# The recurrence's outputs ahead of the last 96 query products, with closer levels

## The chip, the cores and the metric

The kernel runs on one core of a Trainium2 chip. Its time is the device time of one execution in microseconds (us). Five engines run side by side, each with its own queue of instructions in a fixed order: TensorE (PE, matrix products; its weight loads are listed as PEld), VectorE (DVE), ScalarE (ACT), GpSimd (POOL) and SyncE (SP, which here only issues transfers). They meet through semaphores: an instruction that waits holds up everything behind it on its own engine.

## The reference, cut to what matters

The program is one layer of a residual block on 256 tokens of width 1024: a SwiGLU feed-forward, a mixing stage with two branches, a cross attention to a memory, and a second feed-forward. The change lies in the mixing stage, of which these are the two branches:

```python
q_a, f_a, i_a, g_a, q_b, k_b, v_b, f_b, gates = jnp.split(h @ w_in[l], IN_OFFSETS, axis=-1)
o_a = hgrn2_chunkwise(q_a, f_a, i_a, lb_all[l])           # gated linear recurrence, 8 heads of 128
o_a = rmsnorm(o_a, hg_norm_g[l]) * jax.nn.silu(g_a)
o_b = fox_attention(q_b, k_b, v_b, f_b + fox_f_bias[l])   # softmax attention with a forget gate
...
# fox_attention: per block of 128 queries
s = jnp.einsum('bhqd,bhkd->bhqk', qi, k32) * scale
s = s + ci[..., None] - c[:, :, None, :]                  # c: running sum of log forget
p = jax.nn.softmax(jnp.where(kpos <= qpos, s, -jnp.inf), axis=-1)
```

The recurrence's output at a token is a sum over earlier tokens of a decayed query-key product times the input. The attention needs its own queries, keys, values and the running sum `c`.

## The kernel before, in words

Weights come as tiles of 128 x 1024. Each is split by `load_split` into a rounded part `hi` (a copy on ACT, line 136) and a remainder `lo` (a subtraction on DVE, line 137); a projection makes three products per block (hi x hi, hi x lo, lo x hi). Four tiles make a chunk. There are eight buffers each of `hi` and `lo`, two chunks, so a chunk's split can begin when the chunk two before it has been used.

Every product issued through `MM` is noted in a list `log`; transposes are not. `r0` is the length of that list before the gate projection. From `r0` follow, in program order, 144 products of the recurrence's gate (`g_a` with the forget logits, moving width 344), then four chunks of 96 products each (moving width 256): k_b and q_b for heads 0 to 3, k_b and q_b for heads 4 to 7, 528 in all. The column projections `proj_col2` fill one of two `mm` banks of PSUM with 48 products, and DVE empties it (line 996).

The recurrence is computed in nine levels with block sizes 0, 1, 2, 4, 8, 16, 32, 64 and 128. A level of each of two groups of four heads makes some small products into an `acc` bank (`products`), multiplies the running decays into q and k on DVE (`grow`, lines 915 to 925), and keeps the wanted part of the products (`keep`, by DVE below 32, by ACT from 32 on). A level's products read the q and k that the level before has left, and `grow` overwrites what the products have read. So the levels form a chain between PE and DVE.

The framework's planner sets the order on each engine from program order, priorities and data dependences. `with after(n)` gives the instructions inside high priority and places each of those on PE behind product `n` of the list. In this way the levels, which stand behind all 528 products in program order, are woven between them: the nine numbers of `R_AT` say behind which product, counted from `r0`.

Behind the 528 products, in program order and with no such mark, come the recurrence's outputs: for each half `h` of the tokens 8 or 16 products of the kept matrices with the inputs `iv` into two of the four `acc` banks, the norm (`rstd_x`: four squares on ACT for both halves, a chain of eight tiny operations each on DVE), and a multiplication into the gate `Gt` (line 1026). Then POOL fetches the running sums by broadcast (`cbc`, `cbm`, lines 1030 and 1034) and masks them (line 1036). These take buffers of a pool of 20 that the recurrence's q and k gave up. Then two transposes (line 1042) and a copy on DVE (line 1043) lay the running sums in columns, `ct`. Then `fox_scores` makes the attention's scores into two `tr` and four `acc` banks and the softmax, and the v_b projection follows on PE.

Of the kernel before, what the change touches and what calls it, by code (L numbers as in the profile page):

```python
# [16 lines left out]
P = 128  # L17
# [24 lines left out]
L_Y = 16  # L42
M_O = (24, 36)

R_AT = (18, 66, 114, 166, 226, 286, 346, 390, 430)

WARM = 8

# [29 lines left out]
def block_kernel(ctx: ExitStack, tc: tile.TileContext, wts, head_in, gf_in, x_in, mem_in, memT_in, cols, rows, fbias, masks, out):  # L78
    nc = tc.nc
    V, S, G, PE = nc.vector, nc.scalar, nc.gpsimd, nc.tensor  # L80
# [10 lines left out]
    def MM(*args, **kw):  # L91
        log.append(PE.matmul(*args, **kw).ins)  # L92

    @contextmanager
    def after(i):

        with tc.high_priority(), tc.issue_after(log[min(i, len(log) - 1)]):
            yield
# [3 lines left out]
    def nm(s):  # L102
        count[0] += 1
        return f"{s}_{count[0]}"

    def m4(shape, dt=F32, n="m"):
        return mp.tile(shape, dt, tag="m4", name=nm(n))

    def s1(n=1, dt=F32, name="s"):
        return sp.tile([P, n], dt, tag=f"s{n}", name=nm(name), bufs=16)  # L110

    def acc():
        return pp.tile([P, 512], F32, tag="acc", name=nm("acc"), bufs=4)
# [4 lines left out]
    def trp():  # L118
        return pp.tile([P, 512], F32, tag="tr", name=nm("tr"), bufs=2)
# [86 lines left out]
    ident = cp.tile([P, P], F32, name="ident")  # L206
# [52 lines left out]
    def rstd_x(src):  # L259

        s = s1(2, name="ss2")
        for j in range(2):
            ssq(s[:, j : j + 1], src[j])
        return rstd_of(s)
# [688 lines left out]
    r0 = len(log)  # L953
# [15 lines left out]
    cc = sp.tile([8, T], F32, tag="fz", name="cc", bufs=1)  # L969
# [32 lines left out]
    for li, m in enumerate(LEVELS + (64, 128)):  # L1002
        with after(r0 + R_AT[li]):
            for r in recs:
# [7 lines left out]


    OA = Pair()
    for h in range(2):
        ps = [acc(), acc()]
        for hd in range(8):
            g, i = hd // 4, hd % 4
            isl = slice(i * P, (i + 1) * P)
            o = ps[g][:, isl]  # L1020
            MM(o, ATs[g][:, i, h, :], iv[g][:, h, isl], start=True, stop=(h == 0))
            if h == 1:
                MM(o, A128s[g][:, i, :], iv[g][:, 0, isl], start=False, stop=True)
        r = rstd_x(ps)
        for j in range(2):
            V.scalar_tensor_tensor(out=Gt[h][:, j * 512 : (j + 1) * 512], in0=ps[j], scalar=r, in1=Gt[h][:, j * 512 : (j + 1) * 512], op0=ALU.mult, op1=ALU.mult)


    cbc = m4([P, 8, P], n="cbc")
    G.dma_start(cbc, cd[:, 0:P].partition_broadcast(P))  # L1030
    cbm = []
    for g in range(2):
# [2 lines left out]
        tv = t.rearrange("p h (b s) -> p (h b) s", b=2)  # L1035
        G.affine_select(out=tv, in_=tv, pattern=[[0, 8], [-1, P]], compare_op=ALU.is_ge, fill=BIG, base=0, channel_multiplier=1)
        cbm.append(t)

    ct = s1(16, name="ct")
    pc = trp()  # L1040
    for h in range(2):
        PE.transpose(pc[:, h * 8 : h * 8 + 8], cc[:, h * P : (h + 1) * P], ident[0:8, 0:8])
    V.tensor_copy(ct, pc[:, :16])

    ps_, pT0s, pT1s = {}, [], []

# [365 lines left out]
```

## Time and profile before

| what | us |
|---|---|
| median of three runs | 782.95 (782.57 to 785.86) |
| the profiled execution | 783.57 |
| its span in the profile | 781.8 |
| PE busy | 771.5 |
| DVE busy | 648.9 |
| ACT busy | 472.9 |
| POOL busy | 47.3 |

Times in a timeline count from the span's start. A row of a timeline has the start, the length, the engine, the line, the operation, what is written and read, the shape and how many instructions it stands for; in brackets, how long the engine stood idle before it and what ended that. A product on plain f32 operands is listed as two instructions. The first level after the gate's chunk begins is at 285 us, the last level's products end at 326, and the recurrence's outputs are made from 338 to 343.

### The profile page before, as it was taken

The page shows a single profiled execution, that of the slowest core. Times are in us where ns is not written, and L with a number is a line of the kernel's source. Part 1 is how long each engine was busy: PE and PEld are TensorE (multiplying, and loading weights), DVE is VectorE, ACT ScalarE, POOL GpSimd, SP SyncE. Part 2 cuts the span into 40 slices and gives each one's busy share as a digit, 9 for nine tenths or more (in the row PEclk, how much of TensorE's full clock was granted, in tenths as well). Part 3 has the DMA queues.
Part 4 walks back from the last instruction along what each step waited for, and adds up shares of the span by engine and source line. Part 5 has one row for each costly group of instructions (what it writes and reads, how often), then busy time and mean ns, then how long its engine had stood idle before and what let it go on. Part 6 is the DMA issues. An engine that isn't in the chain of part 4 may idle for free.

```text
span 781.8 us, 13108 instructions
## 1 busy us (share of the span) xinstructions
PE 771.5 (99%) x4984; PEld 666.7 (85%) x4984; DVE 648.9 (83%) x999; ACT 472.9 (60%) x711; POOL 47.3 (6%) x80
## 2 busy tenths in 40 slices
PE   9999999999999999999999999999999999999996
PEld 7888878888899999988888888999888888888885
DVE  7799999999887787778778886997787987888874
ACT  7666676577753445447675434744655767777752
POOL 0000000000121100110001221012110000000000
PEclk9999999999999999999999999999999999999999
DMA  9874648377686563673489999679865199789921
GB/s 344 286 261 160 217 162 308 108 255 283 259 296 227 191 218 110 201 272 120 140 291 335 378 344 342 223 271 381 337 213 191 64 343 387 275 296 339 329 92 55
DMA packets 57390, 193.60 MB, mean 248 GB/s; under 512 B 6248, under 2 KB 9712, under 8 KB 57328
## 3 DMA queue, kind: packets, MB, share of 16 engines
q1 hardware_dynamic: 48080, 159.60, 56.7%
q0 software_dynamic: 9104, 33.04, 11.8%
q8 instruction: 39, 0.64, 0.3%
q14 instruction: 23, 0.19, 0.1%
q10 hardware_dynamic: 144, 0.13, 0.0%
HBM read 174.92 MB, written 17.83 MB: 247 GB/s over the span
## 4 chain that ended last, share of the span: by engine, by line
PE 87%; DVE 8%; issue 3%; ACT 1%; DMA 1%; DVEq 0%; ACTq 0%; SPq 0%
PE mm L92 58%; PE acc L92 24%; PE tr L92 3%; DVE lo L156 2%; DVE lo L137 2%; PE tr L324 1%; PE tr L399 1%; DMA raw<-in_wts_dram 1%; DVE sum L469 1%; DVE wide L500 1%; DVE sum L487 0%; DVE sum L465 0%; ACT hi L155 0%; ACT hi L136 0%; PE tr L1082 0%
## 5 line engine op out<-in xcount | busy, mean ns | idle before, releaser
L137 DVE TENSOR_TENSOR lo<-raw,hi 128x1024 fp32r<-128x1024 f32 (+1 forms) x220 | 261.3, 1208 | 48.0 <-ACT hi L136 44.6
L136 ACT CAST hi<-raw 128x1024 fp32r<-128x1024 f32 (+1 forms) x220 | 222.6, 1035 | 94.6 <-PE mm L92 51.1
L92 PE MATMUL mm<-lo,hT 128*128 128x512 f32 (+1 forms) x424 | 161.6, 385 | 0.0
L92 PE MATMUL mm<-hi,hT 128*128 128x512 f32 (+1 forms) x424 | 161.2, 384 | 0.0
L92 PE MATMUL mm<-hi,lT 128*128 128x512 f32 (+1 forms) x424 | 160.9, 384 | 0.0
L92 PE MATMUL acc<-hi,act 128*128 128x512 f32 x352 | 113.2, 390 | 0.0
L92 PE MATMUL mm<-hT,lo 128*128 128x256 f32 x384 | 109.4, 285 | 0.0
L92 PE MATMUL mm<-hT,hi 128*128 128x256 f32 x384 | 108.9, 284 | 0.3 <-issue 0.3
L92 PE MATMUL mm<-lT,hi 128*128 128x256 f32 x384 | 108.9, 284 | 0.0
L92 PEld LDWEIGHTS mm<-hi,hT 128*128 128x128 f32 x424 | 79.6, 188 | 15.1 <-ACT hT L285 0.5
L92 PEld LDWEIGHTS mm<-hi,lT 128*128 128x128 f32 x424 | 79.6, 188 | 14.8 <-DVE lT L286 0.5
L92 PEld LDWEIGHTS mm<-lo,hT 128*128 128x128 f32 x424 | 79.5, 188 | 14.1
L92 PEld LDWEIGHTS acc<-hi,act 128*128 128x128 f32 x352 | 66.0, 188 | 13.6
L92 PEld LDWEIGHTS mm<-hT,hi 128*128 128x128 f32 x384 | 73.6, 192 | 0.5 <-issue 0.5
L92 PEld LDWEIGHTS mm<-hT,lo 128*128 128x128 f32 x384 | 73.6, 192 | 0.2
L92 PEld LDWEIGHTS mm<-lT,hi 128*128 128x128 f32 x384 | 73.6, 192 | 0.1
L92 PE MATMUL acc<-lo,act 128*128 128x512 f32 x176 | 69.1, 393 | 0.0
L155 ACT CAST hi<-wide 128x1024 fp32r<-128x1024 f32 x44 | 45.9, 1055 | 12.8 <-DVE wide L500 7.4
L156 DVE TENSOR_TENSOR lo<-wide,hi 128x1024 fp32r<-128x1024 f32 x44 | 52.5, 1218 | 0.6 <-ACT hi L155 0.2
L794 POOL DMA_DIRECT2D sums<-wide x32 | 23.6, 737 | 347.8 <-DVE wide L791 242.8
L92 PE MATMUL mm<-hi,sh 128*128 128x512 f32 x112 | 43.9, 392 | 0.3 <-ACT keep L529 0.3
L92 PE MATMUL mm<-lo,sh 128*128 128x512 f32 x112 | 43.8, 391 | 0.2 <-DVE lo L156 0.2
(249 smaller groups left out, 1159.6 us busy)
## 6 DMA issues: line engine op xcount, KB each, us to landing
raw<-in_wts_dram SPq DMA_DIRECT2D x228, 512.0 KB, 5.4
sums<-wide POOLq DMA_DIRECT2D x32, 512.0 KB, 6.1
wide<-sums SPq DMA_DIRECT2D x32, 512.0 KB, 6.1
wide<-in_wts_dram POOLq DMA_DIRECT2D x28, 512.0 KB, 6.9
wide<-in_wts_dram SPq DMA_DIRECT2D x16, 512.0 KB, 6.4
raw<-in_gf_dram SPq DMA_DIRECT2D x12, 344.0 KB, 5.6
head<-in_head_dram SPq DMA_DIRECT2D x8, 388.0 KB, 6.0
grow<-in_rows_dram SPq DMA_DIRECT2D x4, 512.0 KB, 7.0
```

What stands on the lines that cost most here:

```text
L92: log.append(PE.matmul(*args, **kw).ins)
L136: S.copy(h, r)
L137: V.tensor_tensor(out=l, in0=r, in1=h.bitcast(F32), op=ALU.subtract)
L155: S.copy(hi, src)
L156: V.tensor_tensor(out=lo, in0=src, in1=hi.bitcast(F32), op=ALU.subtract)
L324: PE.transpose(ps[:, j * P : (j + 1) * P], src(kb), ident)
L399: PE.transpose(trv[:, j, h * P : (h + 1) * P], ats[c, h][:, j * P : (j + 1) * P], ident)
L469: V.tensor_tensor(out=t4[:, i], in0=t2[:, i], in1=raws[i][:, 512:], op=ALU.add)
L500: V.tensor_tensor(out=W[:, :, 0], in0=W[:, :, 0], in1=W[:, :, 1], op=ALU.add)
L794: G.dma_start(sums[u][2 * e : 2 * e + 2, q, :, i * 512 : i * 512 + 512].rearrange("k p n -> p k n"), W[:, e])
```

## The change

The outputs become a function `rec_out(h)`, called for the first half behind product 432 and for the second behind product 456, counted from `r0`. Product 432 is the first of the last query chunk, so 95 of its 96 products are then still to come. The last six levels are tied to earlier products: the distances between the nine become 48, 48, 46, 46, 46, 46, 44 and 40, from 48, 48, 52, 60, 60, 60, 44 and 40. The two transposes and the copy of `ct` come ahead of the broadcasts in program order. No instruction is added or taken away.

```diff
-R_AT = (18, 66, 114, 166, 226, 286, 346, 390, 430)
+R_AT = (18, 66, 114, 160, 206, 252, 298, 342, 382)
+R_OUT = 432
...
     OA = Pair()
-    for h in range(2):
+    ct = s1(16, name="ct")
+
+    def rec_out(h):
         ps = [acc(), acc()]
         for hd in range(8):
             g, i = hd // 4, hd % 4
...
+    with after(r0 + R_OUT):
+        rec_out(0)
+    with after(r0 + R_OUT + 24):
+        rec_out(1)
+    pc = trp()
+    for h in range(2):
+        PE.transpose(pc[:, h * 8 : h * 8 + 8], cc[:, h * P : (h + 1) * P], ident[0:8, 0:8])
+    V.tensor_copy(ct, pc[:, :16])
+
...
-    ct = s1(16, name="ct")
-    pc = trp()
-    for h in range(2):
-        PE.transpose(pc[:, h * 8 : h * 8 + 8], cc[:, h * P : (h + 1) * P], ident[0:8, 0:8])
-    V.tensor_copy(ct, pc[:, :16])
```

## The prediction

> **What bounds the kernel now.** I read the page's busy shares first, then a table of stretches around the changed place, then who waited for whom, then the chain.
>
> ```profile
> span 781.8 us, 13108 instructions
> PE 771.5 (99%) x4984; PEld 666.7 (85%) x4984; DVE 648.9 (83%) x999; ACT 472.9 (60%) x711; POOL 47.3 (6%) x80
> ...
> 284.00:323.00 39.00, 38.72 (x745) 37.49 (x744) 30.02 (x57) 17.76 (x29) 0.54 (x1) 1.00 0.47 153
> 323.00:343.00 20.00, 20.00 (x174) 20.00 (x172) 12.29 (x15) 10.19 (x16) 5.23 (x7) 1.00 0.69 233
> 343.00:353.00 10.00, 9.23 (x50) 7.76 (x49) 9.79 (x38) 3.62 (x11) 0.00 (x0) 1.00 0.66 247
> 353.00:374.00 21.00, 21.00 (x100) 17.36 (x99) 18.45 (x35) 16.95 (x43) 0.00 (x0) 1.00 0.40 138
> ```
>
> The columns of the last four rows are the stretch, its length, the busy time of PE, PEld, DVE, ACT and POOL, then PE's clock, the DMA share and GB/s. TensorE (PE) is the bound: all its idle time is 781.8 - 771.5 = 10.3 us, and its clock is full. The change only reorders work, so it can win what PE idles near it and lose what PE comes to idle. In the projections (284 to 343) PE stands still 0.28 us in 59. The one visible hole is at 343 to 353, where VectorE (DVE) is full (9.79 of 10) with the recurrence's norms and the attention's first scores together. Behind it, from 353 to 374, PE is full although DVE is nearly so. The waits of the stretch and PE's instructions in the hole:
>
> ```profile
> PE tr L92 <- DVE ct L1043: 0.6, 1, 0.6
> PE acc L92 <- DVE G L1026: 0.2, 1, 0.2
> ...
> 339.73 0.39 PE L92 MATMUL acc<-iv,aux 128*128 128x128 f32 x2
> 339.95 0.39 PE L92 MATMUL acc<-iv,f 128*128 128x128 f32 x2
> ...
> 343.38 1.16 PE L92 MATMUL tr<-k_b,q_b 128*128 128x128 f32 x8
> 345.10 0.49 PE L92 MATMUL tr<-k_b,q_b 128*128 128x128 f32 x2 [0.55 <-DVE ct L1043]
> 345.80 1.99 PE L92 MATMUL acc<-k_b,q_b 128*128 128x256 f32 x8 [0.21 <-DVE G L1026]
> ```
>
> One f32 product of this kind is two instructions and takes 0.22 us (339.73 to 339.95). From 343.38 to 345.80 PE makes five (ten instructions), 1.1 us of work in 2.42: 1.3 us are lost. PE waits first for the copy of `ct`, which frees a transposing bank and stands on DVE behind the first norm's chain, then for the multiplication at L1026, which frees two `acc` banks. That 1.3 us is the whole visible prize.
>
> **The change, part by part.** *The levels.* The levels are tied to products counted from `r0`; the 528 products are 144 of the gate, then 4 x 96 of k_b and q_b. Six of the nine are tied to earlier products, the last (m = 128) to 382 instead of 430. PE's order in the stretch from the chain:
>
> ```profile
> 295.24 7.39 PE mm L92 x60
> 302.63 1.25 PE acc L92 x102
> ...
> 311.79 1.14 PE acc L92 x64
> 312.92 5.46 PE mm L92 x44
> 318.39 1.08 PE acc L92 x32
> 319.47 4.99 PE mm L92 x40
> 324.46 1.79 PE acc L92 x16
> ```
>
> A projection product takes 0.12 us (60 in 7.39). PE's work up to product 432 is the same before and after, since all levels stand ahead of it in both; only their places move, the last 48 products = 5.8 us forward, to 318.7. The cost of this part is what DVE and ACT (ScalarE) cannot follow. A level's `grow` on DVE must end before the next level's products:
>
> ```profile
> 271.57 4.63 DVE L137 TENSOR_TENSOR lo<-raw,hi 128x1024 fp32r<-128x1024 f32 x4 [1.10 <-ACT hi L136]
> ...
> 302.56 1.32 PE L92 MATMUL acc<-q,k 128*32 128x16 f32 x128
> ...
> 303.35 0.69 DVE L920 TENSOR_TENSOR q<-q,tq 128x512 f32<-128x512 f32 x1 [0.63 <-PE acc L92]
> 305.25 0.69 DVE L921 TENSOR_TENSOR k<-k,tq 128x512 f32<-128x512 f32 x1
> ...
> 306.33 0.75 DVE L996 SCALAR_TENSOR_TENSOR q_b<-mm,row 128x256 f32<-128x256 f32 x2
> ...
> 315.39 0.69 DVE L921 TENSOR_TENSOR k<-k,aux 128x512 f32<-128x512 f32 x1
> ```
>
> From the start of level 16's products (302.56) to the end of its last `grow` (305.25 + 0.69) pass 3.4 us. With 46 products between levels the period is 46 x 0.12 + 1.25 = 6.8 us, so DVE may be held 3.4 us by other work first. Shorter distances ran already: 44 products stand behind level 32, whose `grow` ended at 315.39 + 0.69 = 316.1, 4.3 us after its products began at 311.79, and PE went from product to level at 318.39 without a wait; 40 stand behind level 64. DVE is busy 30.0 of 39 us up to 323. Up to 318.7 it must now do the same work (the five `grow`s that gate a next level, the splits of two chunks) less one evacuation pair (0.75): 29.3 of 34.7 us, tighter but inside. Cost taken: 0; bounds 0 and the 5.0 us of the first rival. Its cover is the 3.4 us of slack; without it each us of delay is a us of PE.
>
> *The outputs.* `rec_out(0)` (8 products) stands behind product 432 and `rec_out(1)` (16) behind 456. PE makes the same 24 products, 24 x 0.22 = 5.3 us, in both. Added are breaks: a run of 128-wide f32 products twice cuts into the 256-wide stream. The nearest break in the trace is that of level 128:
>
> ```profile
> 324.30 1.95 PE L92 MATMUL acc<-q,k 128*128 128x128 f32 x16
> 326.00 0.36 PE L92 MATMUL mm<-hT,lo 128*128 128x256 f32 x1
> 326.20 0.28 PE L92 MATMUL mm<-hT,hi 128*128 128x256 f32 x1
> ```
>
> Its 16 products stand at 0.106 us each (324.30 to 326.00), and out of it the next projection product follows after 0.20 us instead of 0.12: 0.1 a break, 0.2 for both. The row shows no loss on the way in; a like one there would make it 0.4. I take 0.4, with ends 0.2 and 0.6.
>
> DVE and ACT carry these for each half:
>
> ```profile
> L1026 DVE SCALAR_TENSOR_TENSOR G<-acc,rstd,G x4: 735/738/750, 345.0 to 350.1; 128x512 f32<-128x512 f32 x4
> L257 ACT ACTIVATE junk<-acc x4: 587/597/598, 339.5 to 343.3; 128x512 f32<-128x512 f32 x4
> ...
> 343.54 0.14 DVE L224 TENSOR_SCALAR y<-v 128x1 int32<-128x1 int32 x1
> 344.81 0.15 DVE L238 TENSOR_SCALAR rstd<-y 128x1 f32<-128x1 f32 x1
> ```
>
> The chain of tiny operations runs from 343.54 to 344.96 with one more 0.2 ahead of it, 1.6 us, and two multiplications of 0.74: 3.1 a half, 6.2 us of DVE in all; ACT has four squares, some 3 us with their reads. They move from 342-351, where DVE is full, to about 328-338, where DVE is busy 12.3 of 20 and ACT 10.2 of 20. New waits: DVE's chain waits for ACT's squares, ACT for PE's outputs. Behind the chain on DVE are the splits (L137) of v_b and the evacuations of q_b; the next user of a `mm` bank needs them 48 products (5.8 us) later, the splits 96. At nothing, then, with those 5.8 us as cover, and at most a chain of 3.1 in it.
>
> PE reaches product 432 at about 326.5 as now, ends `rec_out(0)` at 328.3, `rec_out(1)` at 334.8 and the last query product at 343.4, against 343.1 for the end of the outputs now.
>
> *The start of the attention.* The `acc` banks are then long free: the second wait goes whole, 0.3 to 0.5 us of the 1.3. The copy of `ct` needs its two transposes, which come behind the last query product, and then DVE's queue, with q_b's evacuation (0.75) and a v_b split (1.2) in reach; I give half of the remaining 0.9. What is late next is this same copy, not the outputs. Gain 0.8, ends 0 and 1.3.
>
> *POOL's queue.* The broadcasts `cbc` and `cbm` take the buffers of the recurrence's q and k and so follow the last level:
>
> ```profile
> 325.65 0.93 POOL L1030 DMA_DIRECT2D cbc<-cd  x1 [31.75 <-PE acc L92]
> 326.57 1.11 POOL L1034 DMA_DIRECT2D cbm<-cd  x2
> 336.38 1.09 POOL L1036 TENSOR_SCALAR_AFFINE_SELECT cbm<-cbm 128x1024 f32<-128x1024 f32 x1 [8.70 <-DMA cbm<-cd]
> 338.39 1.10 POOL L1036 TENSOR_SCALAR_AFFINE_SELECT cbm<-cbm 128x1024 f32<-128x1024 f32 x1 [0.93 <-DMA cbm<-cd]
> ...
> 315.99 2.35 DVE L137 TENSOR_TENSOR lo<-raw,hi 128x1024 fp32r<-128x1024 f32 x2
> 336.76 3.81 DVE L137 TENSOR_TENSOR lo<-raw,hi 128x1024 fp32r<-128x1024 f32 x2 [3.85 <-ACT hi L136]
> ```
>
> With the last level they move 5.8 us forward: selects at 330.6 and 332.6, finished at 333.7 instead of 339.5. Their first reader is at 344 or later, so no time is won. Two splits beside these selects took 3.81 us against 2.35 for two others, 1.46 more; this slowing moves along and falls where DVE has room: 0, or 1.5 if it meets a late chain.
>
> [...]
>
> **Sum.** Levels 0, breaks +0.4, start of the attention -0.8, POOL 0: -0.4 us. The profiled execution took 783.57 us (its span of 781.8 and 1.8 around it) and would take 783.2. The median shown, 782.95, lies 0.6 below it; less 0.4 that is 782.5.
>
> **Rivals.** *Slower: DVE falls behind the closer levels.* A chunk's four splits run as one block, 4.63 us (row at 271.57), once in 96 products, about every second level. If an evacuation (0.75) stands there too when the products end, `grow` starts 5.4 us late, 2.0 more than the 3.4 of slack, and PE waits at the next level. Two to three such blocks meet the five gating levels: 2.5 x 2.0 = 5.0 us, 787.5. It decides from 3.4 us of delay on; in the old order the delay behind level 32 was 0.9 (4.3 against 3.4). For it speaks DVE at 29.3 of 34.7; against it, that level products stand ahead by priority and that 44 and 40 products sufficed.
>
> *Both waits vanish and the breaks cost nothing more than 0.2:* 782.95 - 1.3 + 0.2 = 781.9. DVE's freed 6.2 us cannot give more, as PE is full from 353 on.
>
> *Nothing is won:* `ct` is as late as now behind splits and evacuation, and the breaks stay: +0.4 - 0.4 for the banks, 783.0, to 783.5 at most.
>
> [...]
>
> **How the numbers follow.** This kernel's measurement can tell about 0.5%, 3.9 us, from no change: 779.0 to 786.9. The forecast has 0.50, both waits gone 0.13, nothing won 0.12, shared port 0.07: all within the bound, with 0.01 for others, 0.83. DVE falling behind has 0.14, slower. Faster by more than 3.9 us has 0.03, since PE idles less than that in the whole neighbourhood. The range is 780.8 (both waits gone, and 1.1 for the scatter of the runs, 782.57 to 785.86) to 787.0 (part of the first rival).
>
> **What would show it.** Right: level 128's products start near 318.7, `G` multiplications (L1026) before 340, no wait of PE for G, the wait for `ct` smaller, cbm's selects near 331. Wrong: PE waits for DVE `q` or `k` ahead of a level or for an evacuation between 284 and 343, or PE idles for a split at v_b's first products. A different order of the loads behind it, in the feed-forward stage, would break the forecast too; nothing in the edit touches those.

## The result, and the profile after

The changed kernel takes 781.54 us (median; 780.73 to 783.39), beside 783.6 us for the kernel before, each the median of 22 executions. The ratio is 0.9979 with a 95% interval of 0.9973 to 0.9986, so the change wins 1.65 us by the ratio (1.1 to 2.1); the two medians lie 2.1 apart. Forecast was a gain of 0.4, from 782.95 to 782.5. One later execution of the change, among the eleven taken beside the last experiment, lasted 3408.84 us; no trace of it is kept, and no ratio here counts it.

The page of the changed kernel, its span and busy shares. Lines of the code have moved by one or more: the products stand at L93, the splits at L138, the multiplication into `G` at L1029, the copy of `ct` at L1038, the selects at L1048. The counts of the engines' instructions are those of before; the six instructions more (13114 against 13108) are none of those that count as busy.

```profile
span 780.0 us, 13114 instructions
PE 770.9 (99%) x4984; PEld 667.1 (86%) x4984; DVE 649.8 (83%) x999; ACT 473.6 (61%) x711; POOL 49.1 (6%) x80
```

Its table of stretches (stretch, length, busy time of PE, PEld, DVE, ACT and POOL, PE's clock, DMA share, GB/s):

```profile
284.00:323.00 39.00, 38.53 (x731) 37.56 (x720) 29.64 (x55) 17.78 (x30) 2.57 (x4) 1.00 0.49 157
323.00:343.00 20.00, 20.00 (x171) 19.85 (x170) 14.35 (x30) 9.08 (x15) 5.05 (x4) 1.00 0.63 224
343.00:353.00 10.00, 10.00 (x54) 8.73 (x55) 9.83 (x27) 5.72 (x17) 0.00 (x0) 1.00 0.54 185
```

The hole at 343 to 353 is closed: PE is busy 10.00 us of 10 there, 9.23 before. DVE has as much to do in that stretch as before (9.83 against 9.79), but PE no longer waits for it. From 323 to 343 DVE has taken over the outputs (14.35 against 12.29). All that the wait view has left for PE from 284 to 400 (us in total, times, longest):

```profile
PE mm L93 <- issue: 0.5, 1, 0.5
```

Its timeline around the start of the attention, first PE, then POOL and DVE:

```profile
318.01 1.17 PE L93 MATMUL acc<-q,k 128*128 128x128 f32 x9
...
342.63 0.28 PE L1037 MATMUL tr<-ident,cc 8*128 8x8 f32 x2
342.84 1.16 PE L93 MATMUL tr<-k_b,q_b 128*128 128x128 f32 x8
343.84 1.89 PE L93 MATMUL acc<-k_b,q_b 128*128 128x256 f32 x8
345.56 1.05 PE L93 MATMUL tr<-k_b,q_b 128*128 128x128 f32 x8
...
361.15 1.03 PE L325 MATMUL tr<-ident,G 128*128 128x128 f32 x8
...
327.82 4.03 POOL L1048 TENSOR_SCALAR_AFFINE_SELECT cbm<-cbm 128x1024 f32<-128x1024 f32 x2 [6.42 <-DMA cbm<-cd]
...
328.99 1.91 DVE L138 TENSOR_TENSOR lo<-raw,hi 128x1024 fp32r<-128x1024 f32 x1
331.00 0.86 DVE L227 SCALAR_TENSOR_TENSOR t<-v,y 128x1 f32<-128x1 f32 x1
...
333.00 1.41 DVE L1029 SCALAR_TENSOR_TENSOR G<-acc,rstd,G 128x512 f32<-128x512 f32 x2
336.80 1.41 DVE L1029 SCALAR_TENSOR_TENSOR G<-acc,rstd,G 128x512 f32<-128x512 f32 x2
...
344.48 0.16 DVE L1038 COPY ct<-tr 128x16 f32<-128x16 f32 x1
```

Level 128 starts at 318.01, both multiplications are over before 340, and from the first score product to the first transpose of `G` PE needs 361.15 - 342.84 = 18.31 us. Two rows of the timeline of the kernel before, the copy of `ct` and that transpose of `G`:

```profile
344.88 0.17 DVE L1043 COPY ct<-tr 128x16 f32<-128x16 f32 x1
...
363.01 1.03 PE L324 MATMUL tr<-ident,G 128*128 128x128 f32 x8
```

There the distance was 363.01 - 343.38 = 19.63 us, so 1.3 us are won in this stretch of the two profiles. I call this distance the start of the attention below. Note where the copy of `ct` stands: 1.64 us behind the first score (344.48 against 342.84), no earlier than before (344.88 against 343.38). The copy did not become faster. With the `acc` banks free, PE makes four score products in them (eight instructions, from 343.84) behind its first four into the `tr` banks, and goes back to the `tr` banks, one of which the copy has to free, only at 345.56.

What is left is one stop of 0.5 us, put down to `issue`: PE waited for nothing that the profile shows.

### The profile page after: what moved, and what is told of

Its sections match the earlier page's. It is cut to its first block, busy times and chain, and to the rows that moved or that the text cites. A ratio compares the mean times of both kernels' runs of the same rounds, so it can differ in the third digit from the quotient of the medians.

```text
span 780.0 us, 13114 instructions
## 1 busy us (share of the span) xinstructions
PE 770.9 (99%) x4984; PEld 667.1 (86%) x4984; DVE 649.8 (83%) x999; ACT 473.6 (61%) x711; POOL 49.1 (6%) x80
## 4 chain that ended last, share of the span: by engine, by line
PE 95%; DVE 4%; issue 1%; ACT 0%; DVEq 0%; ACTq 0%
PE mm L93 62%; PE acc L93 27%; PE tr L93 4%; DVE lo L157 2%; PE tr L325 1%; PE tr L400 1%; PE tr L1088 0%; DVE sum L488 0%; DVE sum L470 0%; DVE sum L466 0%; DVE wide L501 0%; PE tr L1179 0%; PE tr L1285 0%; PE tr L411 0%; DVE at L421 0%
## 5 line engine op out<-in xcount | busy, mean ns | idle before, releaser
L138 DVE TENSOR_TENSOR lo<-raw,hi 128x1024 fp32r<-128x1024 f32 (+1 forms) x220 | 260.8, 1204 | 45.8 <-ACT hi L137 42.3
L93 PE MATMUL mm<-lo,hT 128*128 128x512 f32 (+1 forms) x424 | 161.8, 385 | 0.0
L93 PE MATMUL mm<-hi,hT 128*128 128x512 f32 (+1 forms) x424 | 161.5, 384 | 0.0
L93 PE MATMUL mm<-hi,lT 128*128 128x512 f32 (+1 forms) x424 | 160.8, 384 | 0.0
L93 PE MATMUL acc<-hi,act 128*128 128x512 f32 x352 | 113.3, 391 | 0.0
L93 PE MATMUL mm<-hT,lo 128*128 128x256 f32 x384 | 109.3, 285 | 0.5 <-issue 0.5
L93 PE MATMUL mm<-lT,hi 128*128 128x256 f32 x384 | 109.3, 285 | 0.0
L93 PE MATMUL mm<-hT,hi 128*128 128x256 f32 x384 | 109.0, 284 | 0.0
L93 PEld LDWEIGHTS mm<-hi,hT 128*128 128x128 f32 x424 | 79.7, 188 | 15.1 <-ACT hT L286 0.5
L93 PEld LDWEIGHTS mm<-hi,lT 128*128 128x128 f32 x424 | 79.6, 188 | 14.9 <-DVE lT L287 0.5
L93 PEld LDWEIGHTS mm<-lo,hT 128*128 128x128 f32 x424 | 79.5, 188 | 14.1
L93 PEld LDWEIGHTS acc<-hi,act 128*128 128x128 f32 x352 | 66.0, 188 | 13.5
L93 PEld LDWEIGHTS mm<-hT,lo 128*128 128x128 f32 x384 | 73.7, 192 | 0.7 <-issue 0.7
L93 PEld LDWEIGHTS mm<-lT,hi 128*128 128x128 f32 x384 | 73.7, 192 | 0.2
L93 PEld LDWEIGHTS mm<-hT,hi 128*128 128x128 f32 x384 | 73.7, 192 | 0.1
L93 PE MATMUL acc<-lo,act 128*128 128x512 f32 x176 | 69.2, 393 | 0.0
L93 PE MATMUL mm<-hi,sh 128*128 128x512 f32 x112 | 44.0, 392 | 0.5 <-ACT keep L530 0.5
L93 PE MATMUL mm<-lo,sh 128*128 128x512 f32 x112 | 43.9, 392 | 0.2 <-DVE lo L157 0.2
```

The lines of the kernel that those rows point to most:

```text
L138: V.tensor_tensor(out=l, in0=r, in1=h.bitcast(F32), op=ALU.subtract)
```

## The experiments

**The kernel before, again.** No edit.

> The kernel before, unchanged, for a second profile. In the first one PE stood 0.79 us in the middle of level 1's products (at 267.4) and 0.28 us at 306.3, both put down to issue, with nothing it waited for. If these belong to the program, they stand at the same instructions again; if they are chance, they are elsewhere or gone, and about 0.5 us of the 1.8 us between the two profiled spans is chance too. The two waits at the start of the attention (0.55 for ct, 0.21 for G) should stand as they did.

Measured: 783.4 us in one run, its span 781.6. Its start of the attention lasts 362.74 - 343.82 = 18.92 us, not 19.63, as its timeline shows (POOL, DVE, PE):

```profile
336.76 1.09 POOL L1036 TENSOR_SCALAR_AFFINE_SELECT cbm<-cbm 128x1024 f32<-128x1024 f32 x1 [8.64 <-DMA cbm<-cd]
338.91 2.10 POOL L1036 TENSOR_SCALAR_AFFINE_SELECT cbm<-cbm 128x1024 f32<-128x1024 f32 x1 [1.06 <-DMA cbm<-cd]
...
337.20 2.86 DVE L137 TENSOR_TENSOR lo<-raw,hi 128x1024 fp32r<-128x1024 f32 x2 [3.85 <-ACT hi L136]
340.65 1.44 DVE L137 TENSOR_TENSOR lo<-raw,hi 128x1024 fp32r<-128x1024 f32 x1
...
344.61 0.17 DVE L1043 COPY ct<-tr 128x16 f32<-128x16 f32 x1
...
343.82 1.50 PE L92 MATMUL tr<-k_b,q_b 128*128 128x128 f32 x10
...
362.74 1.03 PE L324 MATMUL tr<-ident,G 128*128 128x128 f32 x8
```

So the prize that the prediction read from one execution, 1.3 us, is not a constant. It differs with how the splits fall against the selects: the two splits took 2.86 us here and 3.81 there, and the hole is 0.6 here and 1.3 there. Here the second select was stretched too, to 2.10 us. Of the two stops put down to `issue`, the one in level 1's products stands at the same instruction again (1.5 us here, 0.8 in the first profile), and the other, 0.3 us, is gone.

**Only the levels.**

```diff
-R_AT = (18, 66, 114, 166, 226, 286, 346, 390, 430)
+R_AT = (18, 66, 114, 160, 206, 252, 298, 342, 382)
```

> The nine levels at their new places, the outputs left behind the 528 products. If the gain is the closed hole at the start of the attention, it is 0 here, within 0.3 us: both waits of PE (ct, G) stay. If closer levels gain by themselves (earlier broadcasts, earlier buffers), it is 0.5 us or more below before. If DVE could not follow closer levels, PE shows waits for q or k before a level and the time is 1 to 5 us above.

Measured: 781.8 us beside 783.44, ratio 0.9975 (0.9958 to 0.9993). The levels alone win as much as the whole change, as far as the intervals can tell, and the start of the attention is 361.17 - 342.86 = 18.31 us, although the outputs still stand behind the last query product and their multiplications begin only at 343.06. Its timeline (DVE, POOL, PE):

```profile
327.65 3.27 DVE L137 TENSOR_TENSOR lo<-raw,hi 128x1024 fp32r<-128x1024 f32 x2
336.19 2.36 DVE L137 TENSOR_TENSOR lo<-raw,hi 128x1024 fp32r<-128x1024 f32 x2 [3.80 <-ACT hi L136]
...
342.96 0.17 DVE L1043 COPY ct<-tr 128x16 f32<-128x16 f32 x1
343.06 1.41 DVE L1026 SCALAR_TENSOR_TENSOR G<-acc,rstd,G 128x512 f32<-128x512 f32 x2
...
328.76 1.09 POOL L1036 TENSOR_SCALAR_AFFINE_SELECT cbm<-cbm 128x1024 f32<-128x1024 f32 x1 [7.36 <-DMA cbm<-cd]
330.13 1.75 POOL L1036 TENSOR_SCALAR_AFFINE_SELECT cbm<-cbm 128x1024 f32<-128x1024 f32 x1 [0.28 <-DMA cbm<-cd]
...
342.64 0.28 PE L1042 MATMUL tr<-ident,cc 8*128 8x8 f32 x2
342.86 1.38 PE L92 MATMUL tr<-k_b,q_b 128*128 128x128 f32 x10
...
361.17 1.03 PE L324 MATMUL tr<-ident,G 128*128 128x128 f32 x8
```

With the levels, the selects have moved from 336-339 to 329-332. They now stretch a pair of splits (3.27) that nothing waits for; the pair ahead of the norm's chain is back at 2.36, and the chain, with the copy of `ct` behind it, ends 1.4 us sooner against the first score: 0.10 us after it, where it was 1.50.

**Only the outputs.** The change with the old `R_AT`.

> The old places of the levels, the outputs behind products 432 and 456, so right behind the last level at 430. If the outputs' place alone makes the gain, this is as fast as the change, 1.3 to 1.7 us below before, with no wait of PE for ct or G. If the closer levels are needed to make room, PE waits for the copy of level 128's products (L950, some 1 us) ahead of the second half, or DVE comes late to the scores, and half the gain or less is left.

Measured: 782.26 us, ratio 0.998 (0.9964 to 0.9995). The start of the attention is again 18.31 us (343.27 to 361.59). Either half of the change closes the hole and the two don't add up. The outputs do it in the way seen in the profile after: the chain and the multiplications are done long before the scores.

**The copy of `ct` early, all else as before.**

```diff
+    ct = s1(16, name="ct")
+    pc = trp()
+    with after(r0 + 300):
+        for h in range(2):
+            PE.transpose(pc[:, h * 8 : h * 8 + 8], cc[:, h * P : (h + 1) * P], ident[0:8, 0:8])
+        V.tensor_copy(ct, pc[:, :16])
```

> The kernel before, with the two transposes of the running sums and the copy of ct placed behind product 300, so that nothing waits for ct; the outputs stay behind the 528 products. If the two waits add up, the ct wait goes and 0.6 to 0.7 us are won. If they stand one behind the other on the same chain of DVE (the norm of the first half), PE gets through the transposing bank's products and then waits for G instead, from about 344.1 to 345.6, and 0.2 us are won at most.

Measured: 783.69 us, ratio 0.9996 (0.998 to 1.0012): nothing. In its wait view for PE, from 339 to 400, the wait has only changed its name:

```profile
PE acc L92 <- DVE G L1033: 1.5, 1, 1.5
```

In its timeline (DVE, PE) the splits ahead of the chain are as slow as before, and the start of the attention lasts 365.63 - 345.62 = 20.01 us:

```profile
339.30 3.81 DVE L137 TENSOR_TENSOR lo<-raw,hi 128x1024 fp32r<-128x1024 f32 x2 [3.85 <-ACT hi L136]
...
345.62 1.28 PE L92 MATMUL tr<-k_b,q_b 128*128 128x128 f32 x10
...
365.63 1.03 PE L324 MATMUL tr<-ident,G 128*128 128x128 f32 x8
```

The two waits of the hole, for `ct` and for `G`, stand one behind the other on the same late chain of DVE. Taking the first away lengthens the second.

**The selects only write.** POOL's two selects become fills; this leaves the mask and the keys' running sums out of the scores.

```diff
-        G.affine_select(out=tv, in_=tv, pattern=[[0, 8], [-1, P]], compare_op=ALU.is_ge, fill=BIG, base=0, channel_multiplier=1)
+        G.memset(tv, 0.0)
```

> The kernel before, with the two selects on POOL that mask the running sums replaced by fills of the same tiles, which take their place on POOL but read nothing; the mask and the keys' running sums are left out of the scores. Every other instruction keeps its place. The theory after the first four runs: in the kernel before, these selects slow the splits that stand on DVE ahead of the first norm and of the copy of ct (3.81 and 2.86 us for two splits in two profiles, against 2.36), and this makes the hole. Then two splits take 2.4 us here, PE waits neither for ct nor for G, its stretch from the first score to the first transpose of G is 18.3 us as with closer levels (19.6 and 18.9 before), and the time is 0.6 to 1.3 us below before. If the hole comes from the norm's place on DVE alone, the stretch stays above 18.9 and the time within 0.3 us of before.

Measured: 782.8 us beside 783.17, ratio 0.9989 (0.9978 to 1.0), a gain of 0.9 us by the ratio whose interval reaches no gain at all. So the time alone does not show the forecast 0.6 to 1.3 us; the trace has to decide. It is that of the slowest of the twelve executions, 785.38 us, with a stop of 2.6 us far ahead of this place (the last section comes back to it). The order of everything else is that of the kernel before, and so are the places of the fills, but in its timeline (POOL, DVE, PE) the splits keep their length:

```profile
339.48 0.96 POOL L1036 MEMSET cbm<- 128x1024 f32 x1 [8.66 <-DMA cbm<-cd]
341.32 0.96 POOL L1036 MEMSET cbm<- 128x1024 f32 x1 [0.88 <-DMA cbm<-cd]
...
339.89 2.36 DVE L137 TENSOR_TENSOR lo<-raw,hi 128x1024 fp32r<-128x1024 f32 x2 [3.84 <-ACT hi L136]
...
346.65 0.17 DVE L1043 COPY ct<-tr 128x16 f32<-128x16 f32 x1
...
346.52 1.38 PE L92 MATMUL tr<-k_b,q_b 128*128 128x128 f32 x10
```

The start of the attention is 18.31 us (346.52 to 364.83), and PE waits neither for `ct` nor for `G`. This settles the cause of the hole: POOL's selects, which read where the fills only write, slow DVE's splits and so hold up the chain that PE waits for. The five profiles stand in order, by what the splits ahead of the chain take beyond 2.36 and 1.22 us, and by the start of the attention beyond 18.31 us:

| kernel | splits, excess us | start of the attention, excess us |
|---|---|---|
| only the levels | 0.0 | 0.0 |
| selects only write | 0.0 | 0.0 |
| before, again | 0.5 + 0.2 | 0.6 |
| before | 1.45 | 1.3 |
| `ct` early | 1.45 | 1.7 |

The last starts the scores sooner against the chain, since the two transposes of `cc` are out of the way.

**Levels 36 and 28 products apart.** The change with the last seven levels closer still.

```diff
-R_AT = (18, 66, 114, 160, 206, 252, 298, 342, 382)
+R_AT = (18, 66, 114, 150, 186, 222, 258, 294, 330)   # the one
+R_AT = (18, 66, 114, 142, 170, 198, 226, 254, 282)   # the other
```

> The changed kernel with 36 products between the last six levels (150 to 330). A level's period is 36 x 0.12 + 1.25 = 5.6 us against 3.4 us from a level's first product to the end of its grow. If 3.4 us is the price of a level, 2.2 us of slack are left, PE waits nowhere or once for under 1 us, and the time is that of the change within 0.5 us. If the change is already near DVE's limit, PE waits for q or k at several levels and the time is 2 to 5 us above the change.

> The changed kernel with 28 products between the last six levels (142 to 282). The period is 4.6 us, the slack 1.2 us, less than one split (1.2) and an evacuation (0.75) together. Expected by the slack: waits of PE for q or k before three to five levels, 0.5 to 1.5 us each, 2 to 5 us above the change. If DVE still follows, the time is that of the change.

Measured: 783.7 us at 36 (ratio 1.001, 0.9997 to 1.0023) and 783.47 at 28 (1.0009, 0.9992 to 1.0026), beside 783.17. Both lose the gain of the change, but not in the way the first rival has it. This is all that the wait view has for PE from 257 to 347, first at 36, then at 28:

```profile
PE acc L93 <- issue: 1.4, 2, 1.1
```

```profile
PE mm L93 <- issue: 1.3, 1, 1.3
PE acc L93 <- issue: 0.6, 2, 0.3
```

There is no wait for DVE, whose `grow` kept up even at 28 x 0.12 + 1.25 = 4.6 us a level, so the expected waits for q and k did not come. The start of the attention is 18.31 us in both. What is left to see are the stops put down to `issue`, 1.4 and 1.9 us. The two profiles are of executions of 782.48 and 782.83 us, about the fastest of their kernels; where the rest of the lost gain goes in the slower ones no trace shows.

**The change, again.** No edit.

> The changed kernel once more, for a second profile. If its place of the levels shortens the stops put down to issue, those between level 1 and the last query product are under 0.7 us again (0.6 in the first profile, 1.4 and 1.7 in the two of before). If these stops are chance, any value from 0.3 to 2 may stand here. The stretch from the first score to the first transpose of G is 18.3 us again.

Measured: 782.93 us in one run, span 781.2, with the start of the attention at 18.31 us and stops of 1.5 us, by its wait view for PE:

```profile
PE acc L93 <- issue: 1.5, 2, 1.3
```

So these stops, 0.5 us in one execution of the change and 1.5 in another, explain 1.0 of the 1.2 us between the two spans, and its place of the levels does not keep them short. Counting PE's instructions (products, weight loads and the semaphore instructions between them) gave a place for them: each begins at an instruction whose number leaves 193 when divided by 256. PE's products and weight loads, 2 x 4984, are 38.9 times 256, and the page of the change lists 39 instruction transfers (queue `q8`: packets, MB), 16 KB each:

```profile
q8 instruction: 39, 0.64, 0.3%
```

A block of 256 instructions lasts 15 us where PE makes projection products alone. A level below 64 is 256 instructions in 1.25 us, and a block that holds most of a burst is passed in 2 to 4 us. That gave the last theory, that PE stops where it passes a block before the next has come.

**Levels set by the block borders.** Three kernels on one chip, the blocks reckoned from the rows' durations: one whose bursts leave every block at 4.6 us or more, one at distances of 42 to 50 that puts the bursts of levels 1 and 8 into blocks of 2.3 and 2.0 us, and the change, whose shortest blocks are 3.2 and 3.5 us.

```diff
-R_AT = (18, 66, 114, 160, 206, 252, 298, 342, 382)
+R_AT = (19, 76, 113, 150, 211, 253, 297, 341, 381)   # no short block
+R_AT = (18, 60, 102, 144, 186, 236, 286, 336, 380)   # two short blocks
```

> The change with the levels behind products 19, 76, 113, 150, 211, 253, 297, 341 and 381. Counted in the traces so far, every stop of TensorE that is put down to issue between the first level and the last query product stands at an instruction whose number on TensorE leaves 193 when divided by 256, that is at a border of blocks of 256 instructions, and an instruction transfer of 16384 bytes runs in each of them. A level below 64 is 256 instructions in 1.25 us; where its burst falls, a block is passed in as little as 3.2 us (the change's block at level 1, 3.5 at level 8), against 6 to 8 us for one without a burst's half. Theory (instruction blocks): TensorE stops where it passes a block before the next has arrived. Here no block takes less than 4.6 us by the rows' durations, so the stops between levels 1 and 128, 0.63 and 1.82 us in the two profiles of the change, fall below 0.5 us together, and the time to 0.5 to 1.0 us below the change in the same call (ratio to the kernel before about 0.997). Rival (the stops come by chance, whatever the blocks): stops of 0.6 to 1.8 us as before and the time of the change within 0.3 us.

> The change with the levels behind products 18, 60, 102, 144, 186, 236, 286, 336 and 380: distances of 42 to 50, as in the change, where no wait on VectorE grew even at 28. Theory (instruction blocks): the bursts of level 1 and of level 8 fall so that the block in which each stands is passed in 2.3 and 2.0 us by the rows' durations, so two stops of 1 to 2.5 us, at those two places, and a time 1 to 2.5 us above the change in the same call. Rival (the distance between the levels decides, through VectorE): no wait on VectorE and the time of the change within 0.3 us.

> The change itself, as the yardstick for the other two on the same chip: a ratio of 0.998 to the kernel before. Theory (instruction blocks): its stops between levels 1 and 128 lie at the blocks of level 1 and level 8. Rival (chance): anywhere.

Measured, beside 783.38 us for the kernel before: without short blocks 780.92 us (ratio 0.997, 0.9959 to 0.9981), with two 782.71 (0.9991, 0.9982 to 1.0), the change 781.61 (0.9976, 0.9966 to 0.9986). The table of stretches without short blocks:

```profile
257.00:285.00 28.00, 28.00 (x660) 27.09 (x659) 23.02 (x35) 15.10 (x19) 2.28 (x6) 1.00 0.66 218
285.00:345.00 60.00, 60.00 (x806) 58.81 (x805) 45.39 (x88) 28.93 (x46) 7.35 (x8) 1.00 0.55 183
```

With two:

```profile
257.00:285.00 28.00, 26.83 (x648) 25.78 (x647) 21.64 (x31) 14.32 (x19) 2.27 (x6) 1.00 0.62 211
285.00:345.00 60.00, 59.81 (x809) 58.75 (x808) 44.87 (x87) 28.29 (x46) 6.49 (x8) 1.00 0.56 179
```

Its chain, in order of time (start, length, what):

```profile
266.77 1.17 issue
...
290.87 0.19 issue
```

The change's first stretch, where it idles 0.20 us, its only stop:

```profile
257.00:285.00 28.00, 27.80 (x628) 26.82 (x628) 22.58 (x33) 15.04 (x19) 2.27 (x6) 1.00 0.66 219
```

Without short blocks PE is busy 88.00 us of 88 and the wait view is empty. With two, the chain shows exactly two stops, in the bursts of level 1 (266.77) and level 8 (290.87). The two kernels differ only in where the same bursts stand, and by 1.8 us, with intervals that just do not touch. This is the theory's order and places. The sizes are less sure: the second stop was expected at 1 us or more and was 0.19; the kernel with two short blocks lies 1.1 us above the change and the one without 0.7 below it, and both intervals overlap that of the change. The change itself has no stop at level 8's block here. The kernel without short blocks is the fastest of the kernels run.

## Why the prediction came out as it did

The direction was right, but the gain of 1.65 us is four times the forecast 0.4. That the forecast time of 782.5 is only 1.0 above the measured one is in part luck: it starts from 782.95, the median of three executions, where 22 give 783.6. By its own steps:

- *The levels, at 0.* That DVE follows was right, with room to spare: no wait at 46, 36 or 28 products, and the first rival (787.5) fell. Forecasting nothing won from them was wrong. By themselves they won as much as the whole change (ratio 0.9975), since the selects move with the last level and leave the splits that the chain waits for.
- *POOL's queue, at 0.* Here is the step that failed. The prediction had the rows, two splits at 3.81 instead of 2.35 us beside the selects, and wrote that the slowing "moves along and falls where DVE has room". It priced only where the slowing goes (+1.5 if it meets a late chain), and never asked what it was costing where it was: those splits stood ahead of the norm's chain, and their 1.46 us were the 1.3 us hole. The traces show the slowing where POOL's instruction reads and writes, and none where it only writes: the two splits took 3.81 and 2.86 us beside the selects in the two profiles of before, and 2.36 with fills in their place. That a shared port is the cause, as the name in the chances has it (0.07), no run shows; the case that the name stands for, PE waiting for a slowed split after the change, did not come (no such wait from 284 to 400). In the changed kernel the slowing is still there (a split of 1.91, a tiny operation of 0.86 against its usual 0.22), on a chain that nothing waits for. The selects came 3 us sooner than the 330.6 forecast, as their transfers did not keep their distance from the last level.
- *The start of the attention, at -0.8.* It was -1.3 against the one profile of before and -0.6 against the other; both waits are gone, and the wait that the prediction kept for `ct` (half of 0.9 us) did not come. "What is late next is this same copy" was half right: the copy is as late as ever, but PE has other products to make by then. The rival in which both waits vanish, 781.9, was the nearest of all; it had a chance of 0.13.
- *The breaks, at +0.4.* They cost nothing. From level 128's first product to the transposes of `cc`, with the same products in between, PE takes 342.63 - 318.01 = 24.62 us with the outputs inside the query products, and 342.64 - 318.01 = 24.63 with them behind (the kernel with only the levels moved).
- *Nothing else was in the sum.* The hole gives 0.6 to 1.3 of the 1.65 us, 1.0 as the mean of the two profiles. What remains lies within the stops at block borders, which the prediction did not know. Ahead of the attention they took 1.1 and 1.5 us in the two profiles of before and 0.5, 1.5 and 0.2 in the three of the change, 0.6 less on average. That would make the sum 1.6, but this second part is an estimate from five profiles whose values vary by a microsecond, so its share stays open.

## What to carry to other kernels

When a slowed instruction moves, price both ends: what it will hold up where it goes, and what it is holding up where it stands. When a wait is removed, look at the order behind it, since two waits on one late chain count once, and an engine with other work at hand does not notice a result that is as late as before. Here the first of two waits, removed alone, won nothing (ratio 0.9996), and PE did not stop for a copy that stood 1.64 us behind the first score. One execution's hole is a sample: the same kernel showed 1.3 and 0.6 us.

## What was not expected of the hardware

**PE stops at borders of 256 instructions.** Between 257 and 345 us, the 13 profiles have 23 stops of 0.2 to 2.6 us that are put down to `issue`. All stand at borders of 256 PE instructions, behind blocks that PE passed in 2.4 to 5.8 us (21 of them in under 4 us). Behind longer blocks, up to the 15 us of one of projection products alone, there is none; the shortest hold most of a burst of 256 instructions in 1.25 us. The packets of `q8` in the traces (39 transfers, 0.64 MB, for PE's 38.9 blocks) point to what the stops wait for: each stop ends 0.9 to 1.6 us after the end of the last instruction transfer ahead of it (1.21 and 1.39 in the first profile of before, 1.45 in that of the change), and no border without a stop was passed sooner than 1.4 us after its transfer, counted in order with one transfer to a border. That PE lacks its next instructions there is an inference from these times; no view names what a stop put down to `issue` waits for. The same border stops PE for different times, and its transfer comes at different times: in the three profiles of the change, the one for the border in level 1's burst began 1.1, 1.3 and 2.6 us after PE had passed the border before, and PE stopped there 0, 0.20 and 1.26 us. Why it begins later in one execution than in the next is open.

**Behind a stop of 2.6 us PE's clock was halved.** The profile of the kernel whose selects only write has the longest stop, in the burst of level 1. Its timeline, PE's idle time in brackets:

```profile
270.04 0.41 PE L92 MATMUL acc<-q,k 128*32 128x16 f32 x13 [2.57 <-issue]
```

Its table of stretches right behind:

```profile
270.00:273.00 3.00, 2.96 (x22) 2.92 (x23) 1.93 (x4) 0.55 (x1) 0.95 (x3) 0.50 0.06 19
273.00:276.00 3.00, 3.00 (x21) 3.00 (x20) 1.21 (x2) 2.30 (x3) 0.18 (x1) 0.98 0.00 0
```

Behind the stop the clock column stands at 0.50 for 3 us. Three us at half the clock are, as an estimate, another 1.5 us on top of the 2.6. In the kernel with two short blocks, a stop of 1.17 us left the clock at 1.00. Here 2.57 us of standing still, right behind a burst of small products, came before the half clock. It was seen once between 257 and 345 us in these profiles, so what it takes stays open.
